# Hybrid encoder block on one core: weights loaded as two channels per partition, the last expert's rows scattered, one modulation step moved

## The chip, the core and the metric

The kernel runs on one core of a Trainium2 chip. The metric is the device time of one execution in microseconds (us). Engines are named as in the profile: PE (TensorE matmul), DVE (VectorE), ACT (ScalarE), POOL (GpSimd), SP (SyncE, which here only issues DMAs).

## What is computed

One layer of an encoder: 512 tokens (S) of width 1024 (D). Everything is float32.

```
mod = silu(c) @ w_ada + b_ada                       # 6 vectors of 1024: shift1, scale1, gate1, shift2, scale2, gate2
h = modulate(rms_norm(x, norm_pre_mix), shift1, scale1);  proj = h @ w_in
mix = concat(rms_norm(windowed_gqa(q, k, v, sink)), rms_norm(spatial_gating(u, v)))
x = x + gate1 * rms_norm(mix @ w_out, norm_post_mix)
h2 = modulate(rms_norm(x, norm_pre_ffn), shift2, scale2)
aff = softmax(h2 @ w_router)                        # 16 experts
gates, idx = top_k(aff.T, 64)                       # each expert picks its 64 tokens
hid = silu(xs @ w_gate) * (xs @ w_up)               # xs: 64 x 1024, w_gate, w_up: 1024 x 2816
y   = scatter_add(idx, (hid @ w_down) * gates)      # w_down: 2816 x 1024
x = x + gate2 * rms_norm(y, norm_post_ffn)
```

The expert weights are 16 x 3 x 1024 x 2816 x 4 bytes = 553.6 MB, and each byte is used once, for 64 tokens.

## The kernel before

**First part (mixing).** Weights of `w_ada`, `w_in` and `w_out` are loaded in pieces into a pool `sl` of six buffers (11,264 bytes per partition each). `mod2(i, kk)` multiplies pieces of `w_ada` by silu(c) on DVE into a sum `racc`; `mod2_cols(i)` (L362) then turns the finished sum into columns: four PE matmuls `pm<-racc,ones`, a DVE copy `rows`, two PE transposes `pt`, and DVE adds of `b_ada`. i = 0 to 3 are gate1, shift2, scale2 and gate2, so `mod2_cols(2)` is the third; it also builds the router's weights `wsp` and the bias row `rb`. Attention runs in 26 steps (L794); the table `todo` hangs other work on a step, and `mod2_cols(2)` hangs on step 1 (L748). A scheduler then interleaves the instructions of each engine; each engine works through its own list in order.

**Expert part.** `route(e)` finds the tokens of expert e by comparing affinities, gathers and transposes them into `XS[e]` (eight blocks of 128 channels by 64 tokens). `hidden` runs `up_proj` for `w_gate` and for `w_up`, with `between()` (the way back of this expert and the routing of the next) written in the middle; `expert` multiplies by `w_down`, and adds the 64 rows to the 512 tokens of `Y` by eight matmuls `pys` with a one-hot matrix. Weights pass through `chunk()` (L810): one DMA by SP of 128 partitions x 2816 floats (11,264 bytes, one channel of `w_gate` or `w_up`, or 2.75 rows of `w_down`) into the next of 13 buffers in the fixed turn `ORDER` (6 of `sl`, 3 of `s2p`, 3 of `s3p`, 1 of `s4p`). An expert is 24 such chunks, and a chunk feeds 6 matmuls. A buffer's DMA is issued when the chunk that lay in it has been multiplied. For expert 0 two more chunks of `w_up` go to places of the first part (`in_places`), so that 15 chunks can be loaded before the first expert starts.

**Pools.** `s2p` and the pool `outw` above it hold weights and tiles of the first part until its end; `s3p` lies where the attention tiles lay. So the first chunks wait for tiles of the first part.

**Last expert.** `last_expert` (L989) loads `w_down` by columns (512, then 256, then 256 columns, the table `LAST`), so its DMAs write runs of 2 KB and 1 KB. `finish` adds each block of columns to `Y`, sums squares and multiplies by gate2; when all have ended, the norm, the residual and five DMAs to `out` follow.

SP issues DMAs in program order, and one that has to wait holds up those behind it. At most eight are under way at once, since eight semaphores take turns.

```
def chunk(ap, shape=(FF,)):
    i = nch[0] % len(ORDER)
    ...
    t = (sl, s2p, s3p, s4p)[ORDER[i]].tile([P] + list(shape), F32, name="w", tag="slot")
    ...
        nc.sync.dma_start(o, i)
```

Of the kernel before, what the change touches and what calls it, by code (L numbers as in the profile page):

```python
# [14 lines left out]
P = 128  # L15
# [14 lines left out]
N1, N2, N3, N4 = 6, 3, 3, 1  # L30
# [24 lines left out]
def encoder_block(ctx, tc, x, c, w_ada, b_ada, norm_pre_mix, norm_post_mix, w_in, sink, sgu_ln_g,  # L55
# [69 lines left out]
    def more_loads():  # L125
        nonlocal wsT, lng, lnb, wst, nsink, wr
        n1 = params(1, (("npf", by_row(norm_pre_ffn[0]), 8), ("pom", by_row(norm_post_mix[0]), 8),
# [28 lines left out]
    ones = cp.tile([P, 40], F32, name="ones")[:, 0:1]  # L156
# [59 lines left out]
    pc = [cp.tile([P, 64], F32, name=f"pc{i}") for i in range(2)]  # L216
# [16 lines left out]
    for o in (8, 32):  # L233
        nc.vector.tensor_scalar(pcol("ba", o, 8), pcol("ba", o, 8), 1.0, None, op0=OP.add)
# [504 lines left out]
    def swap():  # L739
        nonlocal ow, closeO, s2p  # L740
        closeE.close()
        s2p = ctx.enter_context(tc.tile_pool(name="s2p", bufs=N2, side="left", reuse_waits="tile"))
# [5 lines left out]
    at_step(1, (mod2_cols, 2))  # L748
# [155 lines left out]
    CUT = FH + 512  # L904
    KORD = (0, 4, 1, 5, 2, 6, 3, 7)

    def in_places(ap):

        a, b, c = place(0, [2048], F32, "w"), place(1, [2, FF - CUT], F32, "w"), place(5, [2048], F32, "w")
        for i, t in enumerate((a, c)):  # L910
            nc.sync.dma_start(t[:, :CUT], ap[i][:, :CUT])
            nc.sync.dma_start(b[:, i], ap[i][:, CUT:])
        return [(a, b[:, 0]), (c, b[:, 1])]

    def up_proj(e, w, extra=KD):
        pb = [bank("pf") for _ in range(3)]
        ts = {}
        for i, k in enumerate(KORD):
            rows = [w[0, e, kk * P:(kk + 1) * P, :] for kk in KORD[i:i + 2]]
            if i == extra:  # L920
                ts[k], ts[KORD[i + 1]] = in_places(rows)
            elif k not in ts:
                t = chunk(rows[0])
                ts[k] = t, t[:, CUT:]
            for n in range(3):
                for h in range(2):
                    o = h * FH + n * 512
                    t = ts[k][0][:, o:o + NW[n]] if o < CUT else ts[k][1][:, o - CUT:o - CUT + NW[n]]
                    nc.tensor.matmul(pb[n][h * 64:(h + 1) * 64, :NW[n]], XS[e][:, k], t,  # L929
                                     start=(i == 0), stop=(i == KD - 1))  # L930
# [28 lines left out]
    def expert(e, between):  # L959
        hidden(e, between)  # L960
        pd = bank("pd")
        for h in range(2):
            wd = w_down[0, e, h * FH:(h + 1) * FH, :].rearrange("(p j) d -> p (j d)", j=NJ)
            for q in range(4):
                t = chunk(wd[:, q * FF:(q + 1) * FF])
                o = q * FF
                while o < (q + 1) * FF:
                    j, r = divmod(o, D)
                    dh, c0 = divmod(r, 512)
# [95 lines left out]
```

## Time and profile before

| | |
|---|---|
| median of 3 runs | 1526.14 us (1521.67 to 1526.99) |
| the profiled execution | 1526.18 us, of which the span from the first to the last instruction is 1524.1 us |
| bytes moved by DMA | 596.86 MB, mean 392 GB/s over the span |
| busy share of the span | PE 90%, DVE 27%, ACT 12%, POOL 7% |
| w loads of 1408 KB | 374 DMAs, 26.7 to 26.8 us from issue to landing (several are under way at once) |

How to read it: a busy PE is not a PE at its peak, because its matmuls overlap. The span has two parts with different limits, the first part up to about 246 us, and the experts after it. What a change is worth has to be read from the part in which it lies, and from the wait that ends last there.

### The profile page before, as it was taken

What the parts mean: (1) busy time and instruction counts of PE and PEld (TensorE: products, weight loads), DVE (VectorE), ACT (ScalarE), POOL (GpSimd) and SP (SyncE); (2) the same over time, 40 slices, a digit from 0 to 9 for tenths busy, and PEclk for the clock granted to TensorE, in tenths of its full rate; (3) what the DMA queues carried; (4) which work ended last, traced back from release to release, by engine and by line L of the source; (5) the groups of instructions that cost most, each with busy time, mean ns of one, the idle gap of its engine ahead of it and who ended that gap; (6) DMA issues with size and microseconds to landing.
All of it is one profiled execution on the core that took longest, in us unless ns stands there. A gap on an engine that the chain in (4) does not pass through costs nothing.

```text
span 1524.1 us, 17489 instructions
## 1 busy us (share of the span) xinstructions
PE 1374.7 (90%) x7286; PEld 610.7 (40%) x7286; DVE 407.0 (27%) x1001; ACT 185.7 (12%) x402; POOL 106.4 (7%) x136
## 2 busy tenths in 40 slices
PE   7998998999999998989899899889898989898886
PEld 5775763444444342423233333333332424333323
DVE  4588863221303030303021211111110303030104
ACT  3336441000000000000000010000000000000001
POOL 2545300000000000000000000000000000000002
PEclk9999999999999999999999999999999999999998
DMA  9975538999999999999999999999999999999995
GB/s 321 344 237 183 196 163 359 407 428 428 428 429 429 429 428 428 428 429 430 428 429 429 429 429 429 428 429 428 429 429 429 428 429 428 429 429 428 430 393 204
DMA packets 92712, 596.86 MB, mean 392 GB/s; under 512 B 8693, under 2 KB 31961, under 8 KB 44761
## 3 DMA queue, kind: packets, MB, share of 16 engines
q1 hardware_dynamic: 92632, 595.74, 94.4%
q8 instruction: 57, 0.93, 0.2%
q14 instruction: 23, 0.18, 0.0%
HBM read 593.62 MB, written 2.10 MB: 391 GB/s over the span
## 4 chain that ended last, share of the span: by engine, by line
DMA 63%; PE 29%; DVE 5%; ACT 1%; issue 1%; SPq 0%; DVEq 0%; ACTq 0%
DMA w<-in_w_down_dram 23%; DMA w<-in_w_up_dram 20%; DMA w<-in_w_gate_dram 20%; PE pf L929 10%; PE pd L971 4%; PE px L868 1%; PE py L324 1%; PE py L322 1%; PE py L323 1%; PE pys L981 1%; DVE ex L831 1%; PE pd L1011 1%; PE qkp L322 1%; PE qkp L323 1%; PE qkp L324 1%
## 5 line engine op out<-in xcount | busy, mean ns | idle before, releaser
L929 PE MATMUL pf<-w,ex 128*64 128x512 f32 (+1 forms) x3072 | 638.3, 561 | 41.8 <-DMA w<-in_w_up_dram 40.4
L929 PEld LDWEIGHTS pf<-w,ex 128*64 128x64 f32 x3072 | 215.0, 137 | 433.2 <-issue 326.1
L971 PE MATMUL pd<-w,ex 128*64 128x512 f32 (+1 forms) x1440 | 319.9, 563 | 33.7 <-DMA w<-in_w_down_dram 33.7
L971 PEld LDWEIGHTS pd<-w,ex 128*64 128x64 f32 x1440 | 109.5, 136 | 232.7 <-issue 126.2
L947 DVE TENSOR_TENSOR ex<-pf,ex 128x512 f32<-128x512 f32 (+1 forms) x48 | 30.3, 647 | 362.0 <-PE pf L929 362.0
L975 DVE TENSOR_SCALAR ex<-pd,gc 128x512 f32<-128x512 f32 x15 | 11.3, 751 | 378.1 <-PE pd L971 378.1
L887 POOL COPY ex<-ex 128x512 f32<-128x512 f32 x16 | 9.9, 616 | 1147.1 <-DVE ex L885 1147.1
L868 PE MATMUL px<-x_sb,ex 128*64 128x256 f32 x512 | 73.0, 397 | 8.6 <-DVE ex L844 7.4
L899 ACT ACTIVATE ex<-pot 128x512 f32<-128x512 f32 x16 | 9.6, 597 | 545.2 <-PE pot L897 545.2
L987 DVE TENSOR_TENSOR y<-pys,y 128x512 f32<-128x512 f32 x112 | 68.2, 680 | 17.0 <-PE pys L981 17.0
L954 ACT ACTIVATE ex<-pht 128x512 f32<-128x512 f32 (+1 forms) x48 | 23.5, 559 | 374.3 <-PE pht L953 374.3
L981 PE MATMUL pys<-ex 64*128 64x512 f32 x240 | 55.6, 602 | 12.7 <-DVE ex L975 12.7
L880 DVE TENSOR_SCALAR ex<-pxt,mods 128x64 f32<-128x64 f32 x128 | 34.9, 336 | 94.1 <-PE pxt L875 94.1
L868 PEld LDWEIGHTS px<-x_sb,ex 128*64 128x64 f32 x512 | 42.6, 141 | 39.0 <-DVE ex L844 18.5
L831 DVE SCALAR_TENSOR_TENSOR ex<-rt,afs,before 128x512 f32<-128x512 f32 (+2 forms) x65 | 46.7, 718 | 12.3 <-PE rt L838 12.3
L893 DVE COPY gc<-pgc 128x1 f32<-128x1 f32 x16 | 2.5, 158 | 152.8 <-PE pgc L890 152.8
L939 ACT ACTIVATE ex<-pf 128x512 f32<-128x512 f32 (+1 forms) x48 | 27.0, 562 | 121.0 <-PE pf L929 120.3
L360 DVE SCALAR_TENSOR_TENSOR racc<-ada,cs,racc 128x1024 f32<-128x1024 f32 x28 | 41.5, 1481 | 0.3
L981 PEld LDWEIGHTS pys<-ex 64*128 64x128 f32 x240 | 21.9, 186 | 47.1 <-DVE ex L975 25.9
L953 PE MATMUL pht<-ident,ex 128*128 128x128 f32 x176 | 25.8, 295 | 11.7 <-DVE ex L947 11.7
L953 PEld LDWEIGHTS pht<-ident,ex 128*128 128x128 f32 x176 | 22.7, 213 | 22.4 <-DVE ex L947 22.4
L470 POOL TENSOR_SCALAR pr<-pr,dn 128x256 f32<-128x256 f32 (+1 forms) x32 | 26.6, 844 | 38.3 <-DVE dn L468 20.7
(242 smaller groups left out, 1005.7 us busy)
## 6 DMA issues: line engine op xcount, KB each, us to landing
w<-in_w_gate_dram SPq DMA_DIRECT2D x128, 1408.0 KB, 26.8
w<-in_w_up_dram SPq DMA_DIRECT2D x126, 1408.0 KB, 26.7
w<-in_w_down_dram SPq DMA_DIRECT2D x120, 1408.0 KB, 26.7
ada<-in_w_ada_dram SPq DMA_DIRECT2D x16, 1024.0 KB
w<-in_w_down_dram SPq DMA_DIRECT2D x18, 512.0 KB, 9.6
wq<-in_w_ada_dram SPq DMA_DIRECT2D x16, 512.0 KB, 6.0
wi<-in_w_in_dram SPq DMA_DIRECT2D x4, 1024.0 KB, 8.7
wq<-in_w_in_dram SPq DMA_DIRECT2D x8, 384.0 KB, 6.2
```

Of the source, the lines that this page charges most:

```text
L322: nc.tensor.matmul(o, ah, bh, start=start, stop=False)
L323: nc.tensor.matmul(o, ah, bl, start=False, stop=False)
L324: nc.tensor.matmul(o, al, bh, start=False, stop=stop)
L360: nc.vector.scalar_tensor_tensor(acc[i], t[:, r], cs[:, k:k + 1], acc[i], op0=OP.mult, op1=OP.add)
L831: nc.vector.scalar_tensor_tensor(junk[:, :c1 - c0], p[:, c0:c1], afs[:, b, e:e + 1], before[:, o + c0:o + c1], op0=OP.subtract, op1=OP.is_ ...
L868: nc.tensor.matmul(px[i][h * CAP:(h + 1) * CAP, :256], ohr[:, b], x_sb[:, b, c0:c0 + 256], start=(b == 0), stop=(b == NB - 1))
L880: nc.vector.tensor_scalar(xs[:, k], pt[:, c0:c0 + CAP], s2[:, k:k + 1], sh2[:, k:k + 1], op0=OP.mult, op1=OP.add)
L929: nc.tensor.matmul(pb[n][h * 64:(h + 1) * 64, :NW[n]], XS[e][:, k], t, start=(i == 0), stop=(i == KD - 1))
L953: nc.tensor.transpose(p[:, j * P:(j + 1) * P], hv[:, j0 + j], ident)
L971: nc.tensor.matmul(pd[dh * 64:(dh + 1) * 64, c0:c0 + n], hT[:, j, h * CAP:(h + 1) * CAP], t[:, o - q * FF:o - q * FF + n], start=(h == 0 a ...
L981: nc.tensor.matmul(p, OT[e][dh * 64:(dh + 1) * 64, b * P:(b + 1) * P], oe[dh * 64:(dh + 1) * 64, :], start=True, stop=True)
L987: nc.vector.tensor_tensor(yb, p, yb, op=OP.add)
```

## The change

1. **Loads.** `chunk()` now loads 128 partitions x 5632 floats (22,528 bytes: channels 2p and 2p + 1 of a block of 256, or 5.5 rows of `w_down`) into six buffers in the turn `ORDER = (0, 0, 0, 1, 2, 3)`. An expert is 12 such loads, each of which feeds 12 matmuls (11 for `w_down`). The pools `sl` and `s2p` end with the first part, and the six buffers are laid over them; the fifth has 248 floats of padding, so that all six start at a multiple of 1024 bytes (before, the three of `s3p` did not). For expert 0 one pair of channels goes to three places, and one more half pair to a half buffer `w4`.
2. **Channel order.** So that partition p holds channels 2p and 2p + 1, the transposes of x (`x2_cols`, `route`) read every second column, `mod2_cols(1)` and `(2)` write their columns by pairs, and `b_ada` and `norm_pre_ffn` come in by an extra small tile `prm2` and two transposes (`pair_cols`).
3. **Third modulation.** `mod2_cols(2)` hangs on step 5 in place of step 1.
4. **Last expert.** `w_down` of the last expert comes in as that of the others, its last load cut in four. In the middle of `hidden` the kernel finishes all 512 tokens as if the last expert added nothing, and gathers the 64 rows of `Y`, of x and of gate2 that it does touch; SP writes the 512 rows to `out` behind the last weights. After the last matmul only those rows are finished (as 128 half rows), and an indirect DMA by POOL writes them over the others.

```diff
-N1, N2, N3, N4 = 6, 3, 3, 1
+N1, N2 = 6, 3
+RPAD = 248
-LAST = ((0, 512, (0, 2, 4, 6, 8, 10, 11)), (512, 256, (0, 4, 8, 11)), (768, 256, (0, 4, 8, 11)))
-ORDER = (0,) * N1 + (1,) * N2 + (2,) * N3 + (3,) * N4
-XK = len(ORDER) - KD
+ORDER = (0, 0, 0, 1, 2, 3)
+XK = 2 * (len(ORDER) - KD // 2)
...
+    def pair_cols():
+        p = bank("pp")
+        for i in range(2):
+            nc.tensor.transpose(p[:, i * 12:(i + 1) * 12], prm2[:, i::2], ident[:12, :12])
+        nc.vector.tensor_copy(pp, p[:, :24].rearrange("p (i r) -> p i r", i=2))
+        nc.vector.tensor_scalar(pp[:, :, 4:8], pp[:, :, 4:8], 1.0, None, op0=OP.add)
...
-    at_step(1, (mod2_cols, 2))
+    at_step(5, (mod2_cols, 2))
...
-    closeO.close()
-    s4p = ctx.enter_context(tc.tile_pool(name="s4p", bufs=N4, side="left", reuse_waits="tile"))
-    s3p = ctx.enter_context(tc.tile_pool(name="s3p", bufs=N3, side="right", reuse_waits="tile"))
+    for c in (closeO, closeW, closeS):
+        c.close()
+    wp = [ctx.enter_context(tc.tile_pool(name=f"w{i}", bufs=n, side=side, reuse_waits="tile"))
+          for i, (n, side) in enumerate(((3, "left"), (1, "left"), (1, "right"), (1, "left")))]
+    w4 = ctx.enter_context(tc.tile_pool(name="w4", bufs=1, side="right", reuse_waits="tile"))
-    def chunk(ap, shape=(FF,)):
+    def chunk(ap, shape=(2 * FF,)):
...
-                nc.tensor.transpose(pt[:, q * P:(q + 1) * P], scr[:, c0:c0 + P], ident)
+                nc.tensor.transpose(pt[:, q * P:(q + 1) * P], scr[:, 256 * i + q:256 * (i + 1):2], ident)
...
+            rows = w[0, e, m * 2 * P:(m + 1) * 2 * P, :].rearrange("(p i) f -> p (i f)", i=2)
+            if j == extra:
+                parts = in_places(rows)
+            elif extra and j > extra:
+                t = w4.tile([P, FF], F32, name="w")
+                nc.sync.dma_start(t, rows[:, :FF])
+                parts = [(t, 0, FF), (chunk(rows[:, FF:], (FF,)), FF, 2 * FF)]
+            else:
+                parts = [(chunk(rows), 0, 2 * FF)]
...
+            if h and tail > 1:
+                cuts[-1:] = [cuts[-2] + (i + 1) * CH // tail for i in range(tail)]
...
+        hidden(e, between)
+        pd = bank("pd")
+        down(e, pd, 4)
         for b in range(NB):
+            nc.sync.dma_start(out[0, b * P:(b + 1) * P, :], Y[b // 2][:, b % 2])
+        yr, yg = oe, hid[:, :S]
+        nc.vector.scalar_tensor_tensor(yr, pd, tg[:, 0:1], Yc, op0=OP.mult, op1=OP.add)
+        sumsq(ss, yr, scr)
+        nc.vector.tensor_tensor(yg, yr, G1c, op=OP.mult)
+        nc.tensor.matmul(pv[:, 0:1], fold2, ss, start=True, stop=True)
...
+        rsqrt(r, v, 1)
+        nc.vector.scalar_tensor_tensor(yr, yg, r, Xc, op0=OP.mult, op1=OP.add)
+        nc.gpsimd.indirect_dma_start(out[0].rearrange("t (h f) -> (t h) f", h=2),
+                                     bass.IndirectOffsetOnAxis(idx[:, 0:1], axis=0), yr, None)
```

The order on SP, where the expert weights begin; before:

```order
L815 DMA w<-in_w_gate_dram 128x2816 x8
L815 DMA w<-in_w_up_dram 128x2816 x5
L911 DMA w<-in_w_up_dram 128x1920
L912 DMA w<-in_w_up_dram 128x896
L815 DMA w<-in_w_down_dram 128x2816 x8
```

and with the change:

```order
L842 DMA w<-in_w_gate_dram 128x5632 x4
L842 DMA w<-in_w_up_dram 128x5632 x2
L938 DMA w<-in_w_up_dram 128x1920 x2
L938 DMA w<-in_w_up_dram 128x1792
L951 DMA w<-in_w_up_dram 128x2816
L842 DMA w<-in_w_up_dram 128x2816
L842 DMA w<-in_w_down_dram 128x5632 x4
```

As many bytes stand ahead of the first reuse of a buffer as before (15 chunks); the first DMA into a used buffer is the second half of the last pair of `w_up`.

The order on PE at the end of the unit `u` of the first part (matmuls `pu`), around the third modulation, which are the matmuls `pb` with their transposes `pt` and, ahead of them, `pm`; `sp`, `ptr` and `po` are attention. Before, its matmuls `pm` stood among those of `pu`, ahead of all of step 1 (they are the ones at 117.44 us of the trace):

```order
L324 MATMUL pu<-wh,hl 128x512
L284 MATMUL pt<-ident,rows_1122 128x128 x2
L277 MATMUL pb<-wr,mods 32x16 x32
L461 MATMUL sp<-qk 128x256 x2
L488 MATMUL ptr<-ident,pr 128x128 x4
L497 MATMUL po<-pT,v_sb 64x256 x4
L552 MATMUL pz<-vn,sgu 128x256 x8
```

and with the change:

```order
L507 MATMUL ptr<-ident,pr 128x128 x4
L339 MATMUL pu<-wh,hl 128x512
L293 MATMUL pm_1293<-racc,ones 32x256 x4
L516 MATMUL po<-pT,v_sb 64x256 x4
L299 MATMUL pt<-ident,rows_1298 128x128 x2
L293 MATMUL pb<-wr,mods 32x16 x32
L480 MATMUL sp<-qk 128x384 x2
L571 MATMUL pz<-vn,sgu 128x256 x8
```

The attention of steps 0 to 4 now stands ahead of the third modulation, between the matmuls of `pu`, and DVE's list has the work on these scores (`pr<-sp`) ahead of the copy `rows` as well.

## Rows read from the trace of the kernel before

**Rows 1.** Busy time of each engine by stretch, with the granted PE clock, the busy share of the 16 DMA engines and what they moved.
```profile
core 0: us, PE busy (x) PEld busy (x) DVE busy (x) ACT busy (x) POOL busy (x), PEclk, DMA share, GB/s
118.00:121.50 3.50, 3.50 (x12) 2.76 (x9) 3.29 (x6) 1.18 (x2) 0.22 (x1) 0.51 1.04 217
247.00:270.00 23.00, 21.64 (x124) 9.02 (x121) 3.62 (x13) 2.55 (x5) 0.00 (x0) 1.00 0.88 361
270.00:300.00 30.00, 29.16 (x161) 11.90 (x159) 5.94 (x18) 2.24 (x5) 0.62 (x1) 1.00 0.98 406
300.00:400.00 100.00, 96.20 (x503) 40.44 (x501) 19.75 (x43) 4.52 (x9) 0.62 (x1) 1.00 1.01 427
500.00:1400.00 900.00, 813.71 (x4101) 311.39 (x4099) 158.27 (x377) 51.18 (x102) 6.78 (x11) 1.00 1.01 429
```

**Rows 2.** The page's chain of work that ended last, as shares of the span by engine.
```profile
DMA 63%; PE 29%; DVE 5%; ACT 1%; issue 1%; SPq 0%; DVEq 0%; ACTq 0%
```

**Rows 3.** SP's timeline: start, time from the first to the last issue of the row, what is loaded, how many DMAs. Several answers of different stretches.
```profile
214.68 20.54 SPq L815 DMA_DIRECT2D w<-in_w_up_dram  x5
...
249.00 0.33 SPq L815 DMA_DIRECT2D w<-in_w_up_dram  x1
251.37 9.78 SPq L815 DMA_DIRECT2D w<-in_w_down_dram  x5
...
265.54 11.14 SPq L815 DMA_DIRECT2D w<-in_w_down_dram  x2
278.71 24.27 SPq L815 DMA_DIRECT2D w<-in_w_gate_dram  x8
304.85 19.21 SPq L815 DMA_DIRECT2D w<-in_w_up_dram  x7
...
829.31 23.76 SPq L815 DMA_DIRECT2D w<-in_w_gate_dram  x8
...
909.89 23.73 SPq L815 DMA_DIRECT2D w<-in_w_gate_dram  x8
...
1451.43 46.19 SPq L815 DMA_DIRECT2D w<-in_w_down_dram  x24
1515.63 4.85 SPq L1030 DMA_DIRECT2D out_dram<-y  x5
```

**Rows 4.** What SP waited for between 100 and 262 us: total, times, longest.
```profile
SPq L815 <- PE py L324: 41.9, 2, 41.5
...
SPq L815 <- DVE ty L786: 13.9, 1, 13.9
```

**Rows 5.** PE's timeline at the start of the experts: start, duration, matmuls (two records for each instruction), in brackets the idle time ahead and what ended it.
```profile
239.41 6.12 PE L868 MATMUL px<-x_sb,ex 128*64 128x256 f32 x32 [1.23 <-DVE rank L852]
...
246.38 19.11 PE L929 MATMUL pf<-w,ex 128*64 128x512 f32 x96
...
273.73 19.11 PE L929 MATMUL pf<-w,ex 128*64 128x512 f32 x96
```

**Rows 6.** PE's timeline in the middle: the end of one expert and the start of the next.
```profile
750.20 7.97 PE L971 MATMUL pd<-w,ex 128*64 128x512 f32 x36
...
772.20 2.79 PE L971 MATMUL pd<-w,ex 128*64 128x256 f32 x12 [0.59 <-DMA w<-in_w_down_dram]
...
779.47 9.67 PE L929 MATMUL pf<-w,ex 128*64 128x512 f32 x48
...
803.28 12.03 PE L929 MATMUL pf<-w,ex 128*64 128x512 f32 x60
```

**Rows 7.** DMA packets in three stretches with all DMA engines busy: 500 to 1400 us (rows of 11,264 bytes), 1476 to 1482 us (2,048 bytes) and 1492 to 1498 us (1,024 bytes). Packets under 512 B are the DMAs' semaphore writes.
```profile
DMA packets 38507, 385.77 MB, mean 429 GB/s; under 512 B 4273, under 2 KB 4273, under 8 KB 4273
...
DMA packets 1195, 2.30 MB, mean 384 GB/s; under 512 B 70, under 2 KB 70, under 8 KB 1195
...
DMA packets 2142, 2.14 MB, mean 356 GB/s; under 512 B 71, under 2 KB 2141, under 8 KB 2141
```

**Rows 8.** PE's timeline around the third modulation.
```profile
114.33 0.40 PE L324 MATMUL pu<-wh,hl 128*128 128x512 f32 x1
117.44 0.64 PE L277 MATMUL pm<-racc,ones 128*32 128x256 f32 x8 [2.71 <-DVE racc L360]
...
118.97 0.63 PE L324 MATMUL pu<-wh,hl 128*128 128x512 f32 x1
```

**Rows 9.** DVE's timeline just after it.
```profile
122.88 0.17 DVE L368 TENSOR_TENSOR mods<-pt,pc 128x8 f32<-128x8 f32 x1 [1.55 <-PE pt L284]
...
124.17 0.49 DVE L463 CUSTOM_DVE_ANT_0 pr<-sp,dist,nsink 128x256 f32<-128x256 f32 x1 [0.43 <-PE sp L461]
```

**Rows 10.** PE's timeline in the last expert: the last chunk of `w_up`, and the last matmuls of `w_down`.
```profile
1474.91 2.58 PE L929 MATMUL pf<-w,ex 128*64 128x512 f32 x12 [0.80 <-DMA w<-in_w_up_dram]
...
1504.96 3.24 PE L1011 MATMUL pd<-w,ex 128*64 128x256 f32 x28
```

**Rows 11.** GB/s of all DMA engines from 1496 to 1516 us, in 40 slices of 0.5 us.
```profile
GB/s 332 352 387 385 383 381 385 375 379 369 258 152 115 90 59 16 0 0 0 0 0 0 0 16 0 0 0 0 0 0 0 0 0 0 0 0 0 0 0 0
```

**Rows 12.** Groups of instructions by shape with their mean duration (ns), from the first part (DVE) and from the last expert (ACT).
```profile
L672 DVE SCALAR_TENSOR_TENSOR ty<-py,rav,ty 128x512 f32<-128x512 f32 x4 | 3.0, 750 | 7.6 <-PE py L324 7.6
...
L213 ACT ACTIVATE ex<-y 128x512 f32<-128x512 f32 x4 | 2.5, 632 | 15.3 <-DVE y L1000 15.2
L213 ACT ACTIVATION_READ_ACCUMULATOR ex<-y 128x1 f32 x12 | 2.2, 186 | 0.0
```

**Rows 13.** The page's smallest load with a landing time, the last number (us from issue to landing).
```profile
nsink<-in_sink_dram SPq DMA_DIRECT2D x1, 4.0 KB, 2.8
```

More of the change, by code (lines that the diff above doesn't have):

```diff
@@ L213, in sumsq @@
         nc.scalar.activation(junk, src, AF.Square, accum_out=dst)
-    pc = [cp.tile([P, 64], F32, name=f"pc{i}") for i in range(2)]
+    pc = [cp.tile([P, n], F32, name=f"pc{i}") for i, n in enumerate((64, 64))]
     def pcol(nm, k, n=1):
@@ L276, in mod_rows @@
         for j in range(4):
-            nc.tensor.matmul(pm[32 * j:32 * j + 32, :n], col.to_broadcast([P, 32]), w[:, j],
-                             start=first, stop=last, tile_position=(0, 32 * j))
+            o = pm[32 * j:32 * j + 32, :n]
+            if len(w.shape) == 4:
+                o = o.rearrange("p (q w) -> p q w", q=w.shape[2])
+            nc.tensor.matmul(o, col.to_broadcast([P, 32]), w[:, j], start=first, stop=last, tile_position=(0, 32 * j))
     def mod_cols(rows, n):
@@ L739, in swap @@
     def swap():
[L740 removed]
+        nonlocal ow, closeO, s2p, closeW
         closeE.close()
[L742 removed]
+        closeW, s2p = phase("s2p", "left", N2)
         closeO, ow = phase("outw", "left")
@@ L902, in encoder_block @@
     NW = [512, 512, FH - 1024]
-    CUT = FH + 512
-    KORD = (0, 4, 1, 5, 2, 6, 3, 7)
+    CUTS = (0, FH + 512, 2 * FH + 1024, 2 * FF)
+    MORD = (0, 2, 1, 3)
     def in_places(ap):
[L909 to L915, printed above, removed]
-        pb = [bank("pf") for _ in range(3)]
[L917 to L930, printed above, removed]
@@ new lines, in in_places, with up_proj @@
+        out = []
+        for i, (c0, c1) in zip((0, 1, 5), zip(CUTS, CUTS[1:])):
+            t = place(i, [2048], F32, "w")
+            nc.sync.dma_start(t[:, :c1 - c0], ap[:, c0:c1])
+            out.append((t, c0, c1))
+        return out
+    def up_proj(e, w, extra=None):
+        pb = [bank("pf") for _ in range(3)]
+        for j, m in enumerate(MORD):
+            rows = w[0, e, m * 2 * P:(m + 1) * 2 * P, :].rearrange("(p i) f -> p (i f)", i=2)
[7 more added lines that the diff above has]
+                parts = [(chunk(rows), 0, 2 * FF)]
+            for i in range(2):
+                for n in range(3):
+                    for h in range(2):
+                        o = i * FF + h * FH + n * 512
+                        t, c0 = next((t, c0) for t, c0, c1 in parts if c0 <= o < c1)
+                        nc.tensor.matmul(pb[n][h * 64:(h + 1) * 64, :NW[n]], XS[e][:, 2 * m + i],
+                                         t[:, o - c0:o - c0 + NW[n]], start=(j == 0 and i == 0),
+                                         stop=(j == 3 and i == 1))
@@ L961, in expert @@
         pd = bank("pd")
[L962 to L969, printed above, removed]
-                    n = min(512 - c0, (q + 1) * FF - o)
-                    nc.tensor.matmul(pd[dh * 64:(dh + 1) * 64, c0:c0 + n], hT[:, j, h * CAP:(h + 1) * CAP],
-                                     t[:, o - q * FF:o - q * FF + n], start=(h == 0 and j == 0),
-                                     stop=(h == 1 and j == NJ - 1))
-                    o += n
+        down(e, pd)
         nc.vector.tensor_scalar(oe, pd, GC[e], None, op0=OP.mult)
@@ new lines, in down @@
+    def down(e, pd, tail=1):
+        for h in range(2):
+            wd = w_down[0, e, h * FH:(h + 1) * FH, :].rearrange("(p j) d -> p (j d)", j=NJ)
+            cuts = list(range(0, NJ * D + 1, CH))
+            if h and tail > 1:
+                cuts[-1:] = [cuts[-2] + (i + 1) * CH // tail for i in range(tail)]
+            for c0, c1 in zip(cuts, cuts[1:]):
+                t = chunk(wd[:, c0:c1], (c1 - c0,))
+                o = c0
+                while o < c1:
+                    j, r = divmod(o, D)
+                    dh, k0 = divmod(r, 512)
+                    n = min(512 - k0, c1 - o)
+                    nc.tensor.matmul(pd[dh * 64:(dh + 1) * 64, k0:k0 + n], hT[:, j, h * CAP:(h + 1) * CAP],
+                                     t[:, o - c0:o - c0 + n], start=(h == 0 and j == 0),
+                                     stop=(h == 1 and j == NJ - 1))
+                    o += n
```

122 lines of the change are left out of this document (72 added, 50 removed).

## The prediction, written before the result was known

> **What bounds the kernel now.** I read the windows first. From 500 to 1400 us the 16 DMA engines are busy 1.01 of the time and move 429 GB/s, with PE at its full granted clock [rows 1]; the chain that ended last is 63% DMA and 29% PE [rows 2]. So the experts are a stream of weights. SP's timeline gives its pace: `w_gate` of two successive experts starts at 829.31 and 909.89, 80.58 us for 24 chunks, 3.36 us each [rows 3]. PE needs 9.67 us for four chunks, 2.42 us each [rows 6]. At 772.20 it waited for the last chunk of `w_down`; the next must land 3.36 us later, at about 775.6, and PE starts it at 779.47, some 4 us behind, because it still has the expert's rows to add to `Y` [rows 6]. It catches up within `w_gate`. Nothing that PE does in an expert's middle sets the time, therefore. Time can come from four places: when the experts start, how the stream gets going again after the first 15 chunks, the rate of the stream, and what stands behind the last weights.
>
> The sum is made against the profiled execution, 1526.18 us (span 1524.1 and 2.1 around it), which agrees with the median of the runs, 1526.14.
>
> **a. The third modulation moves: -2.5 us (0 to -4.4).** Before, PE finishes a `pu` matmul at 114.73 and then stands for 2.71 us until the DVE sum `racc` is there [rows 8]. After that stand, from 118.0 to 121.5, PE's granted clock is 0.51, the 1.2 GHz level [rows 1], and a `pu` matmul takes 0.63 us in place of 0.40 [rows 8]: with 3.5 us at half speed, about 1.7 us more are lost. DVE has 1.55 and 0.43 us of idle time behind it [rows 9], and is busy 3.29 of 3.50 us there [rows 1]. In the new order attention stands ahead of `pm`, so PE has work and DVE has scores to do. PE's loss is 2.71 + 1.7 = 4.4 us, DVE's 2.0. DVE is the fuller, so I take a little over its share, 2.5. The low end is nothing: the same eight kinds of operations come back four steps later, and may make PE stand there. The experts then start at about 244 us, not 246.38 [rows 5].
>
> **b. The stream's start with pairs: +6 us (0 to +9).** Before, all 15 chunks lie in place when PE starts at 246.38 [rows 5]; the first reuse is at 249.00, after one chunk's 19.11 / 8 = 2.39 us [rows 3, 5]. The stream then runs below its pace: (429 - 361) / 429 x 23 = 3.6 us lost from 247 to 270, 1.6 to 300, 0.5 to 400 [rows 1], with 0.6 ahead of 247 about 6.3. After: SP's waits of before, 41.5 us for PE's `py` and 13.9 us for DVE's `ty`, which ended at about 235 with the fifth `w_up` DMA (214.68 + 20.54) [rows 3, 4], concern the same stretch of memory. The order shows that with the change the sixth pair still waits for DVE, and behind it stand the pair in places and the half pair, 5 chunks in all. From 235 to 246.4 pass 11.4 us, enough for 3.4, so nearly two (say 6 us) are missing when PE starts. They don't stop PE, which needs them last, but the stream owes them. Then buffers come free by pairs, every 4.78 us: at 251.2, 256.0, 260.7, 265.5, and, as `w_up` starts at 273.73, again at 278.5, 283.3 and 292.9. The first goes to a half pair (3.36 us), the others to loads of 6.72. From 253 on these end at 256, 263, 270 and 276.5: gaps of 2.0, 1.0 and 0.9 us follow at 278.5, at 292.9 and at the first `w_down`, and each ends with a DMA from a standing start, which for the smallest load took 2.8 us to land [rows 13]; I take 0.8 of it for each. 6 + 3.9 + 2.4 = 12.3, less the 6.3 of before: +6. The low end is nothing missing at the start, the high end three full starts.
>
> **c. The stream's rate: -6 us (0 to -16).** No row of the trace shows a load row above 11,264 bytes, so it is bounded. One of 11,264 bytes costs a DMA engine 11,264 x 16 / 429 = 420.1 ns; at 384 GB/s one of 2,048 bytes costs 85.3 ns and at 356 GB/s one of 1,024 costs 46.0 [rows 7]. Straight lines through two of the three leave 6.7 to 10.9 ns that don't depend on the length. A row of 22,528 bytes would save one of these in each 840 ns, 0.8 to 1.3%, and of some 1250 us of stream that is 10 to 16 us. The other end is nothing: at a share of 1.01 rows of one engine already overlap [rows 1], so that a part or all of the fixed cost may be hidden, or a long row may be cut in two on its way. The short rows speak for a fixed cost, the share above 1 for hiding some of it; I take about the middle, 6.
>
> The Trainium skill ("DMA: Bandwidth & Descriptors", Where 436 GB/s comes from) says two things here. One is a ceiling of 435 GB/s on SBUF's ports: with an estimate from it, 11,264 bytes take 414.3 ns, 5.8 ns are to be had, half of them is 0.69%, and c. would be -8.6, the total 1510. The other speaks against the change: it says that between HBM and SBUF the memory's side, about 358 GB/s, binds, so that longer rows would bring nothing; the 429 of [rows 1] are above that, and the measurement decides.
>
> **d. The last weights: no runs of 2 and 1 KB; e. the end behind them: together -10.8 us (-8 to -12.5).** Before, PE starts on the last chunk of `w_up` as it lands, at 1474.91 [rows 10]. The weights behind it, at 384 and then 356 GB/s [rows 7], come in until the rate falls at about 1503 [rows 11]; PE's last matmuls run from 1504.96 to 1508.20 [rows 10]; `out` is written from 1515.63 to 1520.48 [rows 3], and the span ends at 1524.1, 3.6 after that: 49.2 us in all. After: eight chunks' worth at 3.36 less 0.5% are 26.7 us. PE then has some 3 us left, since its 11 matmuls for a pair, at 0.44 us [rows 6], take 4.9, and a quarter of the pair comes in 1.7. The finish of 128 half rows is one DVE pass from PSUM, 0.75 us, one square with its read, 0.63 + 0.19 [rows 12], one matmul, about seven operations on a column at 0.19 or so, and another pass of 0.75: 4.0 us. The rows of `out` written in between (2 MB, 5.3 us behind the weights) are done by then. The scatter: 3.6 us, as the last DMA of before takes from issue to the end [rows 3], plus 1 for POOL making 128 addresses, a cost that no row shows; SP's issue of 0.33 us [rows 3] is its lower bound, 5 us my upper, a second such DMA with a row for each partition. 26.7 + 3.1 + 4.0 + 4.6 = 38.4, against 49.2: -10.8.
>
> By the Trainium skill (same page, Anatomy of one DMA — SWDGE (gpsimd) path) a POOL DMA has 2.0 us fixed and its bytes at 436 GB/s, for these 256 KB an estimate of 2.6 us; the sum would be 1511. No run shows it yet.
>
> **At nothing:** the transposes with stride (as many as before), `prm2` and `pair_cols` (two transposes, two small DVE operations and one small load, early, with neither PE nor DVE full), and the work in the middle of the last expert, which takes the place of a routing and lies beside 27 us of `w_up` loads. Without that cover it would cost at most its own length, some 8 us, as what stands between `w_gate` and `w_up` takes on PE (246.38 + 19.11 to 273.73) [rows 5].
>
> **Sum:** 1526.2 - 2.5 + 6 - 6 - 10.8 = 1513. Its own range, with b. and c. at half and one and a half times, is 1506 to 1519.
>
> **Rivals.**
> - *The fixed cost is wholly saved.* c. is -14, the total 1505. The lines through short rows are for it, the share above 1 against it. 0.15.
> - *The change does not do what it says:* a long row costs what two cost, and the experts don't start earlier, since DVE is as full four steps later. 1526.2 + 6 - 10.8 = 1521.4. The busy share of 1.01 is for it. 0.17.
> - *The scatter is long:* POOL makes its descriptors one by one, with nothing to hide them, for 8 us more: 1521. Nothing in the trace is for or against it. 0.11.
> - *Slower: the stream starves.* A buffer of a pair comes free only when both channels are used, and there are six in place of thirteen. A pair is held for PE's lag and 4.8 us; the other five cover 33.6 us. It decides when the lag passes 33.6 - 4.8 - 2.8 = 26 us; the trace shows 4 [rows 6]. If it did, one standing start of 2.8 us [rows 13] in each of 15 experts would cost 42: 1555. 0.07.
>
> The forecast has the rest, 0.50. **Bounds:** 0.5%, 7.6 us, is about what a measurement of this kernel can tell from no change: under 1518.5 is faster, over 1533.8 slower. The first rival and nearly all of the forecast are faster, with a small part of the second and third: 0.70; slower is the last, 0.07; the rest, 0.23, the same. The range is 1499 to 1523.
>
> **What would show it.** Right: no stand of PE near 117 us and no clock of 0.5 behind it, first expert matmul near 244; below 400 GB/s until about 300 us, with gaps near 278 and 293; 431 to 433 GB/s from 500 to 1400; from the last `w_up` load's landing to the end 38 us, of which under 5 from the scatter's issue. Wrong: 429 GB/s again (c.), a start at 246 or later (a.), a scatter that runs 8 us or more, or stretches of a DMA share well under 1 in every expert.

## The result and the profile after

The changed kernel takes 1514.91 us (median of 5 runs, 1513.93 to 1517.4), the kernel before 1526.14 (1521.67 to 1526.99): ratio 0.9935, interval 0.9918 to 0.9952. The profiled execution took 1515.3 us, its span is 1513.5, that is 10.6 less than before.

The windows of the kernel after, for the stretches of [rows 1]:

```profile
core 0: us, PE busy (x) PEld busy (x) DVE busy (x) ACT busy (x) POOL busy (x), PEclk, DMA share, GB/s
118.00:121.50 3.50, 3.50 (x16) 2.07 (x16) 3.50 (x11) 2.15 (x4) 1.07 (x3) 1.00 1.00 219
247.00:270.00 23.00, 22.44 (x122) 9.26 (x118) 2.68 (x10) 4.03 (x7) 0.00 (x0) 1.00 1.01 421
270.00:300.00 30.00, 28.33 (x157) 11.93 (x159) 7.93 (x24) 2.24 (x5) 0.62 (x1) 1.00 0.93 381
300.00:400.00 100.00, 96.19 (x491) 36.76 (x489) 19.92 (x44) 4.52 (x9) 0.62 (x1) 1.00 1.00 424
500.00:1400.00 900.00, 805.89 (x4013) 312.57 (x4008) 156.94 (x378) 49.72 (x99) 6.79 (x11) 1.00 1.00 431
```

The stream runs at 431 GB/s in place of 429, and its weak stretch has moved from 247 to 270 us to 270 to 300. The chain that ended last, though, reads quite another way than [rows 2]:

```profile
PE 62%; DMA 30%; DVE 5%; issue 1%; ACT 1%; SPq 1%; POOL 0%; POOLq 0%; ACTq 0%; DVEq 0%
```

PE and DMA have changed places. PE has not become the bound: the DMA share is still 1.00. What has changed is what SP waits for before it can issue a load. From 500 to 1400 us it waited 796 us for earlier DMAs before, and now waits 780 us for PE and 68 for DMAs: with six buffers nearly every load waits for PE to let one go, and the chain follows that wait, however long the load then queues.

The packets of the same 900 us, for which [rows 7] has 38507:

```profile
DMA packets 19402, 388.35 MB, mean 431 GB/s; under 512 B 2151, under 2 KB 2151, under 8 KB 2151
```

Less the small ones that is 17251 packets of 22.5 KB in the mean, so a row of 22,528 bytes goes as one packet and is not cut in two on its way.

SP's timeline (start, time to the row's last issue, what, how many) at the start of the stream, with the first and last `w_gate` row between 500 and 1400 us, which are 11 experts apart:

```profile
221.94 15.66 SPq L842 DMA_DIRECT2D w<-in_w_up_dram  x2
...
253.44 0.33 SPq L842 DMA_DIRECT2D w<-in_w_up_dram  x1
258.16 23.02 SPq L842 DMA_DIRECT2D w<-in_w_down_dram  x4
285.57 21.71 SPq L842 DMA_DIRECT2D w<-in_w_gate_dram  x4
...
507.48 20.61 SPq L842 DMA_DIRECT2D w<-in_w_gate_dram  x4
...
1231.94 20.70 SPq L842 DMA_DIRECT2D w<-in_w_gate_dram  x4
...
1393.45 14.61 SPq L842 DMA_DIRECT2D w<-in_w_gate_dram  x3
```

and some of the same rows before:

```profile
505.46 23.86 SPq L815 DMA_DIRECT2D w<-in_w_gate_dram  x8
...
666.64 23.94 SPq L815 DMA_DIRECT2D w<-in_w_gate_dram  x8
748.70 23.85 SPq L815 DMA_DIRECT2D w<-in_w_gate_dram  x8
...
1235.06 23.88 SPq L815 DMA_DIRECT2D w<-in_w_gate_dram  x8
...
1396.24 25.23 SPq L815 DMA_DIRECT2D w<-in_w_gate_dram  x8
```

(1393.45 - 507.48) / 11 = 80.54 us an expert, and (1396.24 - 505.46) / 11 = 80.98 before. Below "pace" always means this quotient. It has a flaw. In both kernels every third expert takes about 1.5 us more than the others (before, 82.06 us from 666.64 to 748.70, and 80.61 from there to 829.31 [rows 3]); why, no run shows. The eleven experts hold three such long ones before and four after, so the quotients make the gain too small. Nine experts hold three in both: (1235.06 - 505.46) / 9 = 81.07 before and (1231.94 - 507.48) / 9 = 80.50 after, a gain of 0.57 us an expert.

PE's timeline, from the third modulation (`pm`, `pt`) to the first expert, and in the last expert; in brackets the idle time ahead and what ended it:

```profile
128.61 0.66 PE L293 MATMUL pm<-racc,ones 128*32 128x256 f32 x8
...
133.01 0.52 PE L299 MATMUL pt<-ident,rows 128*128 128x128 f32 x2 [2.73 <-DVE rows L383]
...
248.45 19.11 PE L960 MATMUL pf<-w,ex 128*64 128x512 f32 x96
...
1475.15 4.95 PE L960 MATMUL pf<-w,ex 128*64 128x512 f32 x24 [1.72 <-DMA w<-in_w_up_dram]
...
1488.45 5.36 PE L1023 MATMUL pd<-w,ex 128*64 128x512 f32 x22 [0.72 <-DMA w<-in_w_down_dram]
1495.17 9.72 PE L1023 MATMUL pd<-w,ex 128*64 128x512 f32 x50 [1.36 <-DMA w<-in_w_down_dram]
1506.55 0.38 PE L1087 MATMUL pv<-ss,ex 128*128 128x1 f32 x2 [1.66 <-ACT ex L217]
```

The stand of 2.71 us at 117.44 [rows 8] is gone, and one of 2.73 us stands at 133.01. The experts start at 248.45, 2.07 us later than before [rows 5], not earlier. From the last pair of `w_up` at 1475.15 to the end are 38.35 us, where there were 49.2 [rows 3, 10]. The span's change of -10.6 us is thus +2.07 ahead of the experts, 1226.70 - 1228.53 = -1.83 in the stream, and -10.84 in the end.

The end on DVE, ACT and POOL (answers to [rows 12] and to the last row of [rows 3]):

```profile
1504.93 0.75 DVE L1082 SCALAR_TENSOR_TENSOR ex<-pd,ex 128x512 f32<-128x512 f32 x1 [24.16 <-PE pd L1023]
...
1505.77 0.63 ACT L217 ACTIVATE ex<-ex 128x512 f32<-128x512 f32 x1 [22.69 <-DVE ex L1082]
...
1508.52 0.75 DVE L1092 SCALAR_TENSOR_TENSOR ex<-ex,rr 128x512 f32<-128x512 f32 x1
1509.57 1.18 POOL L1093 DMA_INDIRECT out_dram<-ex  x1 [54.51 <-DVE ex L1092]
```

The last matmul ends at 1504.89, the finish takes until 1509.27, and from there to the end are 4.2 us: 0.3 to POOL's start, 1.18 of POOL, 2.75 until the rows have landed.

Where the first part lost its time, on DVE and ACT of the kernel after:

```profile
131.03 1.60 DVE L662 SCALAR_TENSOR_TENSOR wo<-wo,pc 128x1024 fp32r<-128x1024 f32 x1 [2.05 <-POOL wo L659]
132.54 0.41 DVE L383 COPY rows<-pm 128x256 f32<-128x256 f32 x1
```

```profile
119.32 1.28 ACT L613 ACT_TABLE_LOAD   x1
...
122.28 1.28 ACT L485 ACT_TABLE_LOAD   x1
...
128.53 1.28 ACT L613 ACT_TABLE_LOAD   x1
...
136.84 1.28 ACT L485 ACT_TABLE_LOAD   x1 [1.62 <-DVE am L482]
```

The copy `rows`, for which PE stands, is in DVE's list behind an operation on `wo` that waits for POOL. And as attention's exponentials (L485) now stand between the blocks of `us` (L613), ACT changes its table four times here; before it did so twice, as with step 1 below.

### The profile page after: what moved, and what is told of

The parts are those of the page before. It is cut to its first block, busy times and chain, and to the rows that moved or that the text cites. A ratio compares the mean times of both kernels' runs of the same rounds, so it can differ in the third digit from the quotient of the medians.

```text
span 1513.5 us, 16775 instructions
## 1 busy us (share of the span) xinstructions
PE 1365.0 (90%) x7136; PEld 610.8 (40%) x7136; DVE 409.0 (27%) x1001; ACT 188.3 (12%) x399; POOL 109.2 (7%) x132
## 4 chain that ended last, share of the span: by engine, by line
PE 62%; DMA 30%; DVE 5%; issue 1%; ACT 1%; SPq 1%; POOL 0%; POOLq 0%; ACTq 0%; DVEq 0%
PE pf L960 32%; DMA w<-in_w_down_dram 29%; PE pd L1023 8%; PE px L895 4%; PE pys L1001 4%; PE py L339 1%; PE py L337 1%; PE py L338 1%; PE pgc L916 1%; PE qkp L337 1%; DVE ex L858 1%; DMA out_dram<-y 1%; PE qkp L338 1%; DVE ex L995 1%; PE qkp L339 1%
## 5 line engine op out<-in xcount | busy, mean ns | idle before, releaser
L960 PE MATMUL pf<-w,ex 128*64 128x512 f32 (+1 forms) x3072 | 628.4, 559 | 27.3 <-DMA w<-in_w_up_dram 27.3
L960 PEld LDWEIGHTS pf<-w,ex 128*64 128x64 f32 x3072 | 227.5, 137 | 404.0 <-issue 326.8
L1023 PE MATMUL pd<-w,ex 128*64 128x512 f32 (+1 forms) x1414 | 335.2, 594 | 42.4 <-DMA w<-in_w_down_dram 42.4
L1023 PEld LDWEIGHTS pd<-w,ex 128*64 128x64 f32 x1414 | 104.0, 137 | 261.4 <-issue 183.0
L897 ACT ACTIVATE ex<-px 128x256 f32<-128x256 f32 x32 | 12.3, 384 | 138.6 <-PE px L895 138.4
```

Of the source, the lines that this page charges most:

```text
L1023: nc.tensor.matmul(pd[dh * 64:(dh + 1) * 64, k0:k0 + n], hT[:, j, h * CAP:(h + 1) * CAP], t[:, o - c0:o - c0 + n], start=(h == 0 and j == ...
```

## The experiments

Theory of the first part: moving the third modulation costs time by itself. Rival: other edits there (the strided transposes, `prm2`, the new pools) cost it. Theory of the stream: each row has a fixed cost, of which a part is hidden. Rival: the gain comes from where the buffers lie, or from fewer DMAs.

**1. Step 1 again.**

```diff
-    at_step(5, (mod2_cols, 2))
+    at_step(1, (mod2_cols, 2))
```

> The changed kernel with the third modulation hung on step 1 again. Theory (the move itself costs: it made two more ACT table loads and put the copy rows behind a wo operation that waits for POOL): the experts start at about 245.2 us in place of 248.45, the total is about 3.2 lower, 1512. Rival (the other edits of the first part cost it): start still at 248 or later, total 1515.

1512.66 us, ratio to before 0.9912 (0.9895 to 0.9928). The start of an execution varies by 1 to 2 us, so the stretch is better taken between two operations of DVE that all these kernels have, `rs_i<-hv` and `rs_i<-rav`. Before, with step 1:

```profile
110.00 0.16 DVE L192 TENSOR_SCALAR rs_i<-hv 128x4 int32<-128x4 int32 x1
...
146.75 0.15 DVE L192 TENSOR_SCALAR rs_i<-rav 128x4 int32<-128x4 int32 x1
```

The changed kernel with step 5:

```profile
108.80 0.15 DVE L196 TENSOR_SCALAR rs_i<-hv 128x4 int32<-128x4 int32 x1
...
148.91 0.16 DVE L196 TENSOR_SCALAR rs_i<-rav 128x4 int32<-128x4 int32 x1
```

This run, with its first expert matmul:

```profile
108.72 0.15 DVE L196 TENSOR_SCALAR rs_i<-hv 128x4 int32<-128x4 int32 x1
...
144.97 0.16 DVE L196 TENSOR_SCALAR rs_i<-rav 128x4 int32<-128x4 int32 x1
...
244.84 17.61 PE L960 MATMUL pf<-w,ex 128*64 128x512 f32 x88
```

36.75, 40.11 and 36.25 us. The move costs 3.9 us here, and 3.6 at the start of the experts; the other edits cost nothing in this stretch. The theory that the move itself costs holds; by which of its two ways, this run doesn't tell.

**2. The kernel before with step 5**, the same line changed the other way.

> The kernel before with the third modulation on step 5 and nothing else changed. Theory: the experts start at about 249.6 (246.38 + 3.2), total about 1529, with 8 ACT table loads in place of 6. Rival (the prediction's term a): start at about 244, total 1523.6. A third, that later starts are absorbed by the stream: start 249.6, total 1526.

1527.26 us, ratio 1.0018 (1.0009 to 1.0028): slower by about 2 us. The stretch takes 147.28 - 108.56 = 38.72 us against 36.75. The first matmul at 246.25 is no later than before, since this execution came to `hv` 1.4 us earlier; the expected 249.6 was missed for that reason and because PE's stand ahead of `pt` is only 1.09 us here.

**3. Step 3.**

```diff
-    at_step(5, (mod2_cols, 2))
+    at_step(3, (mod2_cols, 2))
```

> The changed kernel with the third modulation on step 3: two pairs of ACT table loads more in its list than with step 5, but no wo operation ahead of the copy rows on DVE. From the variance of the fourth unit of work (hv on DVE) to that of the attention rows (rav) it took 36.25 us with step 1 and 40.11 with step 5. If the table loads are what costs: 42 to 44 us, total 1517 or more. If it is the wait of wo for POOL: 36 to 37.5, total 1512.5.

1517.93 us, 42.43 us for the stretch:

```profile
109.23 0.16 DVE L196 TENSOR_SCALAR rs_i<-hv 128x4 int32<-128x4 int32 x1
...
151.66 0.16 DVE L196 TENSOR_SCALAR rs_i<-rav 128x4 int32<-128x4 int32 x1
```

Its ACT has nine table loads from 95 to 147 us; step 5 has five and step 1 three. Two, then four more at 1.28 us are 2.6 and 5.1 us; the stretch grew by 3.9 and 2.3 more. It goes with the count of table loads and not with the wait of `wo`, which is not in front of `rows` here. That the loads alone cause it isn't shown. The order of all work changes with them, and so does PE's clock: the granted clock was 0.72 from 130 to 134 us and 0.65 from 146 to 150 here, where step 5 has 1.00 in the second stretch, so a part of the 2.3 us may be the clock's (its price is in the last section).

**4. Two rows of 11,264 bytes per load**, DMAs and buffers as they are.

```diff
-                parts = [(chunk(rows), 0, 2 * FF)]
+                two = w[0, e, m * 2 * P:(m + 1) * 2 * P, :].rearrange("(i p) f -> p i f", i=2)
+                parts = [(chunk(two), 0, 2 * FF)]
...
+        wd = w_down[0, e].rearrange("(h p j) d -> p h (j d)", h=2, j=NJ)
+            t = chunk(wd[:, :, q * FF:(q + 1) * FF])
```

> The changed kernel, each load of 22,528 bytes per partition now as two rows of 11,264 bytes (channels p and p + 128, or the two halves of w_down), in the same DMAs and the same buffers; the channels then meet those of other tokens' columns, so the product is another one, of the same size. Theory (a fixed cost for each row, half of it hidden): 429 GB/s from 500 to 1400 in place of 431, an expert 0.45 us longer, total about 1521. Rival (the gain came from fewer DMAs, or from where the buffers lie): 431 GB/s, 1515.

1521.85 us, ratio 0.9974 (0.9965 to 0.9984); 429 GB/s; pace 81.00. The long row is worth 0.46 us an expert (here, too, four of the eleven are long ones). One of the 16 DMA engines has 8 of the 128 rows of a load, 96 in the 12 of an expert: 4.8 ns for each row saved. The rival of fewer DMAs finds nothing: this run has 12 an expert, and over nine experts 80.95 us, against 81.07 before, where runs 2 and 9, with the stream of before, have 81.17 and 81.00.

**5. Buffers off their places.**

```diff
-        t = wp[n].tile([P, 2 * FF + RPAD] if n == 2 else [P] + list(shape), F32, name="w", tag="slot")
-        if n == 2:
-            t = t[:, :shape[0]]
+        t = wp[n].tile([P, 2 * FF + 8], F32, name="w", tag="slot")[:, :shape[0]]
```

> The changed kernel with every buffer 32 bytes longer, so that five of the six and the half buffer start off the multiples of 256 bytes. Theory: no effect, 431 GB/s and 1515, within 1 us. Rival (the rate came from the alignment): 429 GB/s or less, 1521 or more.

1520.45 us, ratio 0.9967 (0.9955 to 0.998); pace 80.87. I had expected nothing; 0.33 us an expert, nearly three quarters of the 0.46 of the long rows, are gone. The rival holds beside the theory.

**6. Both at once** (4 and 5).

> Both of the two runs before at once: two rows of 11,264 bytes per partition in each load, and the buffers off the multiples of 256 bytes; the product is again another one of the same size. Theory A (row length and place of the buffer each cost something of their own): 80.54 + 0.46 + 0.33 = 81.33 us for an expert, total about 1526. Theory B (a row saves its fixed cost only where it is both long and aligned; short rows don't mind the place): 81.0 us, total about 1522.

1530.31 us, ratio 1.005 (1.0032 to 1.0068); pace 81.63, above theory A's 81.33. The windows from 500 to 1400 us of runs 4, 5 and 6:

```profile
500.00:1400.00 900.00, 799.47 (x4074) 311.00 (x4069) 156.89 (x376) 49.73 (x99) 6.79 (x11) 1.00 1.01 429
```

```profile
500.00:1400.00 900.00, 803.50 (x3995) 311.31 (x3993) 155.67 (x376) 49.69 (x99) 6.76 (x11) 1.00 1.00 430
```

```profile
500.00:1400.00 900.00, 793.98 (x4047) 308.78 (x4043) 156.84 (x376) 49.70 (x99) 6.75 (x11) 1.00 1.01 426
```

The place costs 0.33 us with one row and 81.63 - 81.00 = 0.63 with two. With five of six buffers off, that is 0.33 / 80 and 0.63 / 160 rows: 4 ns for each row that starts off its place, in both. The cost goes with rows.

**7 and 8. How far off matters**: buffers 64 and 512 bytes longer (16 and 128 floats in place of the 8 of run 5).

> The changed kernel with buffers 64 bytes longer, so that they start at multiples of 64 bytes, five of six off the multiples of 1024. If what cost 0.33 us per expert is a start off a multiple of 64 bytes: 80.54 us, total 1515. If 256 or more are wanted: 80.87, total 1520.

1517.03 us, ratio 0.9958 (0.9943 to 0.9973), pace 80.76: half-way between the two expectations.

> The changed kernel with buffers 512 bytes longer: three of the six and the half buffer start at an odd multiple of 512 bytes. If only small offsets cost: 80.54 us for an expert, total 1515. If 1024 is wanted: half of the loss, some 80.7, total 1517.5.

1513.67 us, ratio 0.9935 (0.9917 to 0.9953), pace 80.48: nothing lost. A start at a multiple of 512 bytes is as good as one of 1024; multiples of 64 are not all good. Whether 256 would do isn't parted: of the five buffers of run 7 that lie off a multiple of 512, one lies at a multiple of 256.

The first and the last `w_gate` row of each pace, in us:

| run | first | last | pace |
|---|---|---|---|
| 4 | 509.15 | 1400.14 | 81.00 |
| 5 | 508.19 | 1397.79 | 80.87 |
| 6 | 508.68 | 1406.61 | 81.63 |
| 7 | 505.59 | 1393.98 | 80.76 |
| 8 | 505.38 | 1390.66 | 80.48 |
| 9 | 501.67 | 1391.92 | 80.93 |
| 10 | 510.02 | 1399.71 | 80.88 |

Runs 1, 3 and 12, whose stream is that of the kernel after, have 80.55 each, so 0.1 us is about what a pace can tell.

**9. The kernel before, all buffers aligned.**

```diff
+    padp = ctx.enter_context(tc.tile_pool(name="padp", bufs=1, side="right"))
+    padp.tile([P, 248], F32, name="pad")
     s3p = ctx.enter_context(tc.tile_pool(name="s3p", bufs=N3, side="right", reuse_waits="tile"))
```

> The kernel before with its three unaligned buffers of thirteen moved by 992 bytes, so that all start at a multiple of 1024. If each row that starts off a multiple of 512 bytes costs what the runs with pairs show (0.33 us for 96 rows of an engine less a sixth, 4 ns): 44 rows, 0.18 us per expert, 1522.5 in place of about 1525. If the place only matters to rows above 11,264 bytes: 1525, 80.98 us per expert.

1524.41 us against 1523.55 in the same rounds, ratio 1.0003 (0.9994 to 1.0013); pace 80.93 against 80.98. The 4 ns a row are not found here: the paces are too near each other to tell, but the 0.18 us an expert expected would have made the ratio 0.998, which is outside its interval. Whether a row 992 bytes past a multiple of 1024 costs less than those of runs 5 to 7, or 24 loads an expert hide it, stays open; run 10, where buffers 960 bytes past one cost as much as in run 5, speaks against the first. The alignment is no gain over the kernel before, then; it is what the long rows need to keep theirs.

**10. All 512 rows finished at the end.**

```diff
-        hidden(e, between)
+        hidden(e, lambda: route_back(e))
...
+            for dh in range(2):
+                nc.tensor.matmul(p, OT[e][dh * 64:(dh + 1) * 64, b * P:(b + 1) * P], oe[dh * 64:(dh + 1) * 64, :],
...
+                sumsq(ssf[:, dh, b:b + 1], yb, scr)
+                nc.gpsimd.tensor_tensor(yb, yb, G1[:, dh * 512:(dh + 1) * 512], op=OP.mult)
...
+            nc.vector.scalar_tensor_tensor(f, f, r[:, b:b + 1], x_sb[:, b], op0=OP.mult, op1=OP.add)
+            nc.sync.dma_start(out[0, b * P:(b + 1) * P, :], f)
```

> The changed kernel whose last expert takes its weights in the new way (whole rows, last load in four) but finishes all 512 tokens behind the last matmul, with no scatter. It parts d. from e. Theory (e. is most of the 10.8 us): the last matmul ends 3.1 us behind the last landing as now, but then follow eight additions with their squares at about 0.85 us, four passes at 1.3 and the write, 17 to 19 us from the last matmul to the end in place of 8.6: total about 1524. Rival (the longer rows of w_down were most of it): 1517 or less.

1537.4 us, ratio 1.0087 (1.0069 to 1.0106). From the last matmul, at 1511.56, to the end of the span at 1535.0 it takes 23.4 us, against 8.6 with the scatter, and more than the 17 to 19 expected:

```profile
1520.32 0.97 DVE L1046 TENSOR_TENSOR vf<-ssf 128x4 f32<-128x4 f32 x1 [1.89 <-ACT ex L217]
1521.32 1.19 DVE L1047 TENSOR_SCALAR vf<-vf 128x4 f32<-128x4 f32 x1
...
1524.98 0.16 DVE L205 TENSOR_TENSOR rs_t<-rs_t,vf 128x4 f32<-128x4 f32 x1
```

```profile
1515.09 9.83 POOL L1044 TENSOR_TENSOR y<-y,ex 128x512 f32<-128x512 f32 x8 [141.79 <-ACT ex L217]
```

DVE's operations on four columns took up to 1.19 us while POOL multiplied, and 0.16 as soon as it had ended at 1524.92. The scatter's way is worth 14.8 us against this. The kernel before needed less than this run, 1524.1 - 1508.20 = 15.9 us [rows 10]; by its code it finishes its first columns beside the loads of the others. This run also lost 5 us of stream by accident: it leaves out the small tile `ss` of the last expert, which moved five buffers to 64 bytes short of a multiple of 1024, and its pace is 80.88, as in run 5.

**11. A plain store for the scatter.**

```diff
-        nc.gpsimd.indirect_dma_start(out[0].rearrange("t (h f) -> (t h) f", h=2),
-                                     bass.IndirectOffsetOnAxis(idx[:, 0:1], axis=0), yr, None)
+        nc.sync.dma_start(out[0].rearrange("t (h f) -> (t h) f", h=2)[:P], yr)
```

> The changed kernel with the scatter replaced by a plain store of the same 128 half rows by SP to the first 64 rows of the output, so the rows land in other places. The prediction put the scatter at 4.6 us from issue to end, 1 of them POOL's descriptors, against 3.6 for a plain store. If POOL's part is on the path: 0.6 to 1.2 us less from the last DVE operation to the end than the 4.2 of the changed kernel. If not: the same 4.2.

One execution, span 1512.1. DVE's last operation ends at 1508.36 + 0.75 = 1509.11, and the span 2.99 us later, in place of 4.23: 1.2 us less, which is POOL's 1.18 us. POOL's part is on the path.

**12. The last but one load cut as well**, with step 1.

```diff
-                cuts[-1:] = [cuts[-2] + (i + 1) * CH // tail for i in range(tail)]
+                cuts[-2:] = [cuts[-3] + (i + 1) * CH // 2 for i in range(2)] + \
+                    [cuts[-2] + (i + 1) * CH // tail for i in range(tail)]
```

> The third modulation on step 1, and in the last expert the last but one load cut in two besides the last in four. Where PE was 3.1 us behind the last landing because it could not start the third pair of w_down before the whole pair lay there: the last matmul ends 1.3 us behind the last landing, the total is 1.8 us under the run with step 1 alone, 1510.9. If the buffers come free too late for one more load: no gain, 1512.7 or more.

1512.41 us, ratio 0.9925 (0.9911 to 0.9938): no different from run 1.

```profile
1474.06 4.94 PE L960 MATMUL pf<-w,ex 128*64 128x512 f32 x24 [1.70 <-DMA w<-in_w_up_dram]
...
1501.71 1.72 PE L1024 MATMUL pd<-w,ex 128*64 128x384 f32 x6 [0.52 <-DMA w<-in_w_down_dram]
```

PE no longer lags, but waits 0.52 us for the last piece. It ends 29.4 us behind its start on the last pair of `w_up`, and 29.7 in the kernel after: 0.3 gained of 1.8. SP issued the last piece 19.0 us behind that start (at 1493.1), with one piece fewer 12.9 (at 1488.08), as it waits for a buffer. The second expectation holds: the buffers come free too late. Runs 1 and 12 are the fastest seen; run 1 is the simpler.

## Why the prediction was right, and where not

The time lies 1.9 us above the forecast. Term a. had the wrong sign and missed by 4.6 us; c. came out 2.6 us better than put, and the others were near. That the sum stayed so close is in part luck: a. and c. erred in opposite ways.

| term | predicted | measured |
|---|---|---|
| a. third modulation | -2.5 (0 to -4.4) | +2.07 at the experts' start; +3.4 from `hv` to `rav` |
| b. start of the stream | +6 (0 to +9) | +6.7: the stream's -1.83 less c. |
| c. rate of the stream | -6 (0 to -16) | -8.6: 15 experts by 80.50 - 81.07 |
| d. and e. the end | -10.8 (-8 to -12.5) | -10.84 |

**a. failed**, in the step "In the new order attention stands ahead of `pm`, so PE has work and DVE has scores to do". It had, near 117 us: the granted clock from 118.0 to 121.5 is 1.00. But the step priced the place that was left; the place that was reached could, by its low end of nothing, cost no more than the gain. There PE stands for 2.73 us, as the low end allowed, and ACT, which the step doesn't name, loads tables twice more. The order of ACT, which could be read ahead of the run, shows them; I had read PE's and DVE's alone. Runs 1 and 2 show that the move costs more than it gives in both kernels, 3.9 and 2.0 us from `hv` to `rav`, so a time above nothing belonged into the range. Which share of it is the table loads', the wait of `wo` or the clock's stays open.

**b.** held by its mechanism. Of the prefetch, the third piece in places was issued at 238.59 and took 14.9 us to land, at 253.5, and a half pair of 3.4 us is behind it: 8.4 us missing at 248.45, where I had put 6. SP's issues at 253.44, 258.16, about 281 (258.16 + 23.02) and 285.57 are the buffers coming free by pairs, each some 2 us behind the time predicted, as the start is. The signs named for it came in part: the windows are 421 GB/s from 247 to 270, where under 400 was foretold, 381 from 270 to 300, and 424 from there to 400. The measured size is a difference of two sums and no better than 1 or 2 us.

**c.** held by its mechanism, and its size lies within its range. Run 4 shows the fixed cost of a row: 4.8 ns, within the half of 6.7 to 10.9 that was taken, or 0.46 x 15 = 6.9 us. The other 1.7 of the 8.6 are within what the paces can tell. The 80.58 us from which the pace of before was read is one of its shorter experts; the mean is 81.07. What the working lacked is the condition: in run 5 the rows are as long, and nearly three quarters of the 0.46 us are lost, by the place of the buffers. The ceiling of 435 GB/s that the Trainium skill ("DMA: Bandwidth & Descriptors", Where 436 GB/s comes from) states agrees with the 431 of the profile; its other figure, that about 358 binds between HBM and SBUF, does not.

**d. and e.** held term by term: PE ends 29.7 us behind the start on the last `w_up`, predicted 29.8; the finish took 4.4 in place of 4.0; the scatter 4.2 in place of 4.6, with 1.18 for POOL where 1 was put. Parted at the end of the last matmul, d. is 29.74 - 33.29 = -3.55 us, from the start on the last `w_up` [rows 10], and e. 8.61 - 15.90 = -7.29, from there to the end. No run has the one without the other: run 10, meant for that, finishes in a way that neither kernel has.

The rivals: the fixed cost wholly saved (1505) is out, since 4.8 ns is less than the lines gave. Long rows no cheaper is out by run 4, though its other half, that the experts don't start earlier, came true. The scatter was short. Nothing starved: the DMA share from 500 to 1400 us is 1.00 with six buffers. (By its terms the forecast's own range begins at 1507, not 1506.)

## What to carry to other kernels

Where a step is moved, look at every engine's list at the place it goes to, ACT's table loads among them: the move took away a stand of 2.71 us and brought one of 2.73 us and two table loads of 1.28 us. Lay the buffers of long DMA rows at multiples of 512 bytes, and look again whenever a small tile changes, since leaving one out moved five buffers and cost 5 us. When the chain of waits changes from DMA to PE, look at the DMA share and at SP's waits first; a smaller ring of buffers makes the chain go through PE though the transfers still set the pace.

## What was not expected of the hardware

A row that started off a multiple of 512 bytes in SBUF cost 4 ns more than one at it where an expert has 12 loads (runs 5, 6 and 10), and nothing that was found where it has 24 (run 9). A row more or less cost 4.8 ns (run 4).

PE's clock did not always answer a stand alike. In runs 7 and 8 PE stood 2.73 and 2.72 us ahead of `pt`, as in the kernel after, and the granted clock stayed 1.00; in the kernel after it was 0.77 in the 6 us around it, partly at the 1.2 GHz level. The windows of run 7, then of the kernel after:

```profile
130.00:136.00 6.00, 3.90 (x83) 3.00 (x84) 5.08 (x12) 3.87 (x6) 2.36 (x4) 1.00 0.00 1
```

```profile
130.00:136.00 6.00, 3.27 (x74) 1.66 (x70) 3.23 (x7) 3.56 (x6) 3.08 (x3) 0.77 0.00 1
```

The stretch from `hv` to `rav` took 38.99 us there and 40.11 here: the clock is some 1.1 us of it.

The kernel before and run 9 have the same first part, stands of 2.71 and 2.72 us ahead of `pm`, and stretches of 36.75 and 35.74 us (107.49 to 143.23 in run 9). Their windows:

```profile
112.00:126.00 14.00, 11.23 (x114) 7.71 (x112) 11.49 (x28) 7.39 (x16) 4.54 (x5) 0.88 1.02 265
```

```profile
112.00:126.00 14.00, 9.52 (x117) 5.66 (x117) 11.28 (x32) 9.24 (x19) 5.02 (x9) 1.00 0.92 257
```

So the slow clock behind that stand, for which term a. put 1.7 us, cost about 1.0, and it did not come in every execution.
